# An fp32 encoder layer: one 512-column matmul for two of 256 in the up-projection, and one sum of weights made by an accumulating DMA

## The chip, the core and the metric

The kernel runs on one core of one Trainium2 chip. The metric is the device time in microseconds of one execution; the times are medians over several runs. One further execution was taken with the hardware profiler, and every duration, wait and start in this text comes from it. TensorE (PE in the profile) multiplies matrices, with its weight loads on a row of their own (PEld); VectorE (DVE) and ScalarE (ACT) work element by element and alone read TensorE's results out of PSUM; SyncE (SP) and GpSimd (POOL) issue the DMAs. Each engine works through a queue of its own, in order.

## The reference

One encoder layer on 512 tokens of 2048 channels, all in fp32: a normalisation and an input projection, a convolution group and a neighbourhood-attention group side by side, an output projection added to the residual, and then the part that the change touches, a gated feed-forward network with a width-3 depthwise convolution:

```
xn = rms_norm(x, ffn_norm_g[l])
up = jnp.einsum("bsd,df->bsf", xn, w_up[l])              # 2048 -> 2 x 5632
up = depthwise_conv(up, ffn_dw_w[l], ffn_dw_b[l])
gate, val = jnp.split(up, 2, axis=-1)
x = x + jnp.einsum("bsf,fd->bsd", jax.nn.silu(gate) * val, w_down[l])
return rms_norm(x, final_norm_g)
```

The shapes: `x` (1, 512, 2048), `w_up` (2048, 11264), `w_down` (5632, 2048).

## The kernel before

Activations lie with channels on the 128 partitions and the 512 tokens along the free axis, as tiles of 128x512 (`t2`, a pool of 79 buffers). TensorE multiplies fp32 numbers in two parts: a weight block of 128x1024 is split into a high part `whi` (a ScalarE copy, L108) and a low part `wlo` (a VectorE subtraction, L109), and `mm3` (L119 to L121) adds three products: high by high, high by low, low by high. The split blocks have three buffers each; `plan` lists all blocks in order, and `weights()` makes the splits two blocks ahead of the one in use. The raw blocks come through SP's DMA queue into nine buffers of 512 KB (`raw`).

The feed-forward network goes over 44 blocks `f` of 128 hidden channels, in 11 chunks of four (`NCH`, `CH`). For one `f` the gate and the value of all tokens are a product of 2x2 blocks: the weights are split by gate or value and by the parity of the channel tile (`a11`, `a21`, `a22`, `a12`), the activations by the parity of the channel tile and by token half. `up(f)` computes it with seven products instead of eight, of 256 columns each (`H` = 256 tokens). The seven right factors are sums of activations, made once and held split into high and low halves of one 128x512 tile (`comb`, the tiles `xc`, L488 to L491). The seven left factors are made per `f` in `factors`: three of the loaded blocks as they are, and four sums that VectorE adds (L531, L533, L535, L537), three of them in one buffer `ws`. A product is 8 accumulation steps of three matmuls. Its result lies in PSUM (`pu`, 3 buffers, the seventh product in another), is read by ScalarE copies (L576, L577) and VectorE adds (L578 to L585), and makes gate `g` and value `v`. `hidden(f)` scales both (L599, L600; the value's sign is turned there), applies the convolution (`conv3`, one ScalarE pass and two VectorE passes each), silu and the final product (L603).

The down-projection of a chunk runs during the next chunk. After the four `f` of a chunk, `in_two` splits each hidden tile into high and low (`hh`, `hl`, L608 and L609). `down` takes blocks of `w_down` in units; a unit makes two output tiles of 12 matmuls of 512 columns each (`pd`, two PSUM buffers), ScalarE copies each out (`pdc`, L621), and GpSimd issues a DMA that adds it to the running sum in DRAM (`x2d`, L622). In chunk 0 there is no down unit; in chunks 1 to 9 two units follow the seven products of each `f`; in chunk 10 two follow the second `f`, two the third and four the last. A last part multiplies the last chunk's hidden tiles and normalises.

The order of instructions on each engine is made by a scheduler when the kernel is built; pool buffers are handed out as they come free.

Of the kernel before, what the change touches and what calls it, by code (L numbers as in the profile page):

```python
# [30 lines left out]
KD = D // P  # L31
NC_ = CONV // P
NP_ = HEADS // 2
NF = FF // P
U = 8
# [5 lines left out]
H = S // 2  # L41
CH = 4
NCH = NF // CH
# [11 lines left out]
POFF = {}  # L55
# [8 lines left out]
def layer(ctx: ExitStack, tc: tile.TileContext, xT, w_in, w_out, w_up, w_down, par, tab, out):  # L64
    nc = tc.nc
    consts = ctx.enter_context(tc.tile_pool(name="consts", bufs=1))
# [4 lines left out]
    psm = ctx.enter_context(tc.tile_pool(name="psm", bufs=3, space=bass.MemoryType.PSUM))  # L71
# [10 lines left out]
    def t2(name, dt=F32):  # L82
        return tp.tile([P, S], dt, tag="t2k", name=name)

    def t4(shape, name):

        return wpool.tile(shape, F32, tag="raw", name=name, bufs=NR)

    prm = consts.tile([P, NPAR], F32, name="prm")
    nc.sync.dma_start(prm, par)  # L90

    def pc(name, i):
        o = POFF[name] + i
        return prm[:, o:o + 1]
# [6 lines left out]
    def raw_unit(src, n):  # L101
        raw = t4([P, U * P], "raw")
        return raw, nc.sync.dma_start(raw[:, :n], src)

    def parts(raw, n):
        hi = wpool.tile([P, U * P], F32R, tag="whi", name="whi")
        lo = wpool.tile([P, U * P], F32R, tag="wlo", name="wlo")
        i = nc.scalar.activation(hi[:, :n], raw[:, :n], AF.Copy)  # L108
        j = nc.vector.tensor_sub(lo[:, :n], raw[:, :n], hi[:, :n].bitcast(F32))  # L109
        return hi, lo, i, j  # L110

    def unit(src, n):

        return parts(raw_unit(src, n)[0], n)[:2]

    def mm3(ps, w, wk, mh, ml, start, stop):
        hi, lo = w[:2]
        a = slice(wk * P, (wk + 1) * P)
        nc.tensor.matmul(ps, hi[:, a], mh, start=start, stop=False)  # L119
        nc.tensor.matmul(ps, hi[:, a], ml, start=False, stop=False)  # L120
        return nc.tensor.matmul(ps, lo[:, a], mh, start=False, stop=stop)  # L121
# [100 lines left out]
    for step in ORDER:  # L222
        i = next(a_ if step == "a" else q_)
# [207 lines left out]
    p, n = -1, 0  # L431
# [52 lines left out]
    comb = [[] for _ in range(7)]  # L484

    def halves(src, c):

        t = t2("xc", F32R)  # L488
        nc.scalar.activation(t[:, :H], src, AF.Copy)
        nc.vector.tensor_sub(t[:, H:], src, t[:, :H].bitcast(F32))  # L490
        comb[c].append((t[:, :H], t[:, H:]))  # L491

    def after(d, ps):

# [23 lines left out]

    rstd2 = []

    def stats2():
        rstd2.append((yield from rsqrt_steps(acc2, D, "rstd2")))

    def factors(f):

        def make(c):
            if c == 0:
                a[:] = [raw_unit(w_up[f, q], U * P)[0] for q in range(4)] + [t4([P, U * P], "ws")]
            a11, a21, a22, a12, s_ = a
            if c == 1:  # L530
                add(s_, a21, a22)  # L531
            elif c == 2:
                add(s_, s_, a11)  # L533
            elif c == 4:
                add(a21, a21, a11)  # L535
            elif c == 5:
                add(s_, s_, a12)  # L537
            return parts((a11, s_, s_, a12, a21, s_, a22)[c], U * P)[:2]

        a = []  # L540
        return [lambda c=c: make(c) for c in range(7)]

    add = nc.vector.tensor_add

    def down_units(c, i):

        at = [0, 4, 8, 12, 16] if c < NCH - 1 else [0, 0, 4, 8, 16]
        return range(at[i], at[i + 1], U // CH) if c else ()

    def down_weights(f0, d0):  # L550
        return w_down[:, (f0 * KD + d0 * CH) * P:(f0 * KD + d0 * CH + U) * P]

    for c in range(NCH):
        for i in range(CH):
            plan.extend(factors(c * CH + i))
            for d0 in down_units(c, i):
                plan.append(lambda c=c, d0=d0: unit(down_weights((c - 1) * CH, d0), U * P))

    out_half(mb, after)
    steps.append(stats2())  # L560

    def up(f):

        def product(c):
            w = weights()
            ps = (psa.tile([P, S], F32, tag="po", name="pu") if c == 6 else
                  psm.tile([P, S], F32, tag="mm", name="pu"))[:, :H]
# [5 lines left out]
        uu, vv = t2("u"), t2("v")  # L573
        u, t, u2 = uu[:, :H], uu[:, H:], vv[:, :H]
        g, v = t2("g"), t2("vl")
        nc.scalar.activation(u, product(0), AF.Copy)  # L576
        nc.scalar.activation(t, product(1), AF.Copy)  # L577
# [6 lines left out]
        add(g[:, H:], t, product(5))  # L584
        add(v[:, :H], u2, product(6))  # L585
        return g, v

    def conv3(a, n):
        y = t2("uy")
        o = POFF["fww"] + 3 * n  # L590
        nc.scalar.activation(y, a, AF.Identity, scale=prm[:, o + 1:o + 2], bias=pc("fwb", n))
        nc.vector.scalar_tensor_tensor(y[:, 1:], a[:, :S - 1], prm[:, o:o + 1], y[:, 1:], op0=ALU.mult, op1=ALU.add)
        nc.vector.scalar_tensor_tensor(y[:, :S - 1], a[:, 1:], prm[:, o + 2:o + 3], y[:, :S - 1],
                                       op0=ALU.mult, op1=ALU.add)
        return y

    def hidden(f):
        g, v = up(f)
        nc.vector.tensor_mul(g, g, rstd2[0])  # L599
        nc.vector.scalar_tensor_tensor(v, v, -1.0, rstd2[0], op0=ALU.mult, op1=ALU.mult)  # L600
        g, v = conv3(g, f), conv3(v, NF + f)
        nc.scalar.activation(g, g, AF.Silu)
        nc.vector.tensor_mul(g, g, v)  # L603
        return g

    def in_two(g):
        h, l = t2("hh", F32R), t2("hl", F32R)
        nc.scalar.activation(h, g, AF.Copy)  # L608
        nc.vector.tensor_sub(l, g, h.bitcast(F32))  # L609
        return h, l  # L610

    def down(hs, ds):

        for d0 in ds:
            w = weights()
            for d in range(d0, d0 + U // CH):
                ps = psa.tile([P, S], F32, tag="tr", name="pd", bufs=2)
                for k in range(CH):
                    mm3(ps, w, (d - d0) * CH + k, *hs[k], k == 0, k == CH - 1)
                t = t2("pdc")  # L620
                nc.scalar.activation(t, ps, AF.Copy)  # L621
                nc.gpsimd.dma_start(xd[d], t, accum_op=ALU.add)  # L622
# [12 lines left out]
    x2 = []  # L635
# [95 lines left out]
```

## Time and profile before

| | before |
|---|---|
| median of 3 runs | 2103.06 us (2101.43 to 2103.21) |
| the profiled execution | 2101.72 us, span 2099.9 us, granted TensorE clock 0.996 |
| PE / PEld / DVE / ACT / POOL busy | 98% / 88% / 76% / 47% / 7% of the span |
| DMA | 270.90 MB, 129 GB/s over the span |
| feed-forward network | from about 705 us of the span on |

The span runs from the first to the last instruction. "Busy" for TensorE counts each matmul from its start to its modelled end, and matmuls overlap, so neither its share nor its mean is the price of one more matmul; starts in the timeline give that. In a row of a group, the numbers after the first bar are busy time and the mean in ns of one instruction; after the second bar stands the idle time before them and what ended it. In a timeline row the first two numbers are start and length in us, and a bracket at its end gives the idle time before and who ended it. In a row by stretches the engines' busy times stand in the order PE, PEld, DVE, ACT, POOL, then the granted clock, the share of the DMA engines and GB/s.

### The profile page before, as it was taken

The numbers are of one execution on the slowest core, as the hardware profiler recorded it, in microseconds if no ns is written. First come the engines' busy times: TensorE is split into PE (matmuls) and PEld (weight loads), VectorE is DVE, ScalarE is ACT, GpSimd is POOL, SyncE is SP. The second block draws the span as 40 slices with busy tenths as digits, with TensorE's granted clock in tenths as the row PEclk, the third lists the DMA queues.
The fourth block names the chain that finished last, engine by engine and source line by source line (L and its number), as shares of the span: only waits on it lengthen the run. The fifth ranks groups of instructions, "written<-read, shape, count | busy, mean of one in ns | idle before, by whom it ended". The sixth has DMA issues, their size and how long they took to land.

```text
span 2099.9 us, 32453 instructions
## 1 busy us (share of the span) xinstructions
PE 2061.7 (98%) x13024; PEld 1851.1 (88%) x13024; DVE 1585.8 (76%) x2180; ACT 985.3 (47%) x1428; POOL 140.0 (7%) x166
## 2 busy tenths in 40 slices
PE   8999999999999999999999999999999999999997
PEld 6888888877778899999999999999999999999987
DVE  7985796686568898777777778777777777878756
ACT  6234424447436544444444444454454444545452
POOL 0000000000000000110110110110111011010110
PEclk9999999999999999999999999999999999999998
DMA  6333223335324244555555565665565555554672
GB/s 237 101 111 110 81 81 110 101 101 200 116 96 140 71 121 124 138 130 143 130 139 143 122 146 135 132 140 136 137 140 127 144 131 138 144 121 123 147 193 81
DMA packets 95911, 270.90 MB, mean 129 GB/s; under 512 B 10640, under 2 KB 14736, under 8 KB 95760
## 3 DMA queue, kind: packets, MB, share of 16 engines
q1 hardware_dynamic: 72720, 226.88, 33.7%
q0 software_dynamic: 23040, 41.95, 14.7%
q8 instruction: 102, 1.67, 0.3%
q14 instruction: 49, 0.40, 0.1%
HBM read 218.46 MB, written 50.33 MB: 128 GB/s over the span
## 4 chain that ended last, share of the span: by engine, by line
PE 94%; DVE 4%; DMA 1%; ACT 1%; issue 0%; SPq 0%; DVEq 0%; ACTq 0%
PE pu L121 13%; PE pu L119 13%; PE pu L120 13%; PE pd L119 8%; PE pd L120 8%; PE pd L121 8%; PE pj L119 7%; PE pj L121 7%; PE pj L120 7%; PE po L119 2%; PE po L120 2%; PE po L121 2%; DVE wlo L109 1%; PE sc L365 1%; PE po L408 1%; PE trp L395 1%
## 5 line engine op out<-in xcount | busy, mean ns | idle before, releaser
L121 PE MATMUL pu<-xc,wlo 128*128 128x256 f32 x2464 | 697.8, 283 | 2.1 <-DVE wlo L109 2.1
L108 ACT ACTIVATE whi<-raw 128x1024 fp32r<-128x1024 f32 x368 | 389.4, 1059 | 660.0 <-PE pu L120 299.3
L119 PE MATMUL pu<-xc,whi 128*128 128x256 f32 x2464 | 698.3, 283 | 0.8 <-ACT whi L108 0.7
L120 PE MATMUL pu<-xc,whi 128*128 128x256 f32 x2464 | 698.0, 283 | 0.0
L109 DVE TENSOR_TENSOR wlo<-raw,whi 128x1024 fp32r<-128x1024 f32 x368 | 449.1, 1222 | 171.6 <-ACT whi L108 143.9
L121 PEld LDWEIGHTS pu<-xc,wlo 128*128 128x128 f32 x2464 | 473.3, 192 | 3.2 <-DVE wlo L109 3.2
L119 PEld LDWEIGHTS pu<-xc,whi 128*128 128x128 f32 x2464 | 473.5, 192 | 2.9 <-ACT whi L108 1.2
L120 PEld LDWEIGHTS pu<-xc,whi 128*128 128x128 f32 x2464 | 473.6, 192 | 1.9 <-issue 0.2
L109 DVE TENSOR_TENSOR wlo<-ws,whi 128x1024 fp32r<-128x1024 f32 x132 | 161.5, 1223 | 160.2 <-ACT whi L108 159.7
L622 POOL DMA_DIRECT2D x2d<-pdc x160 | 139.3, 873 | 1896.0 <-ACT pdc L621 1893.4
L119 PE MATMUL pj<-xh,whi 128*128 128x512 f32 x640 | 254.1, 398 | 8.5 <-ACT whi L108 8.5
L121 PE MATMUL pj<-xh,wlo 128*128 128x512 f32 x640 | 250.3, 391 | 1.7 <-DVE wlo L109 1.7
L119 PE MATMUL pd<-hh,whi 128*128 128x512 f32 x640 | 249.6, 390 | 1.9 <-ACT pdc L621 1.9
L120 PE MATMUL pj<-xl,whi 128*128 128x512 f32 x640 | 250.3, 391 | 0.0
L108 ACT ACTIVATE whi<-ws 128x1024 fp32r<-128x1024 f32 x132 | 139.9, 1060 | 233.7 <-PE pd L120 142.4
L120 PE MATMUL pd<-hl,whi 128*128 128x512 f32 x640 | 249.5, 390 | 0.0
L121 PE MATMUL pd<-hh,wlo 128*128 128x512 f32 x640 | 249.0, 389 | 0.0
L279 DVE SCALAR_TENSOR_TENSOR y<-ch,prm,y 128x504 f32<-128x504 f32 (+14 forms) x240 | 170.2, 741 | 3.2
L119 PEld LDWEIGHTS pj<-xh,whi 128*128 128x128 f32 x640 | 120.7, 189 | 37.0 <-ACT whi L108 10.5
L121 PEld LDWEIGHTS pj<-xh,wlo 128*128 128x128 f32 x640 | 120.5, 188 | 29.1 <-DVE wlo L109 3.6
L119 PEld LDWEIGHTS pd<-hh,whi 128*128 128x128 f32 x640 | 120.3, 188 | 26.3 <-ACT pdc L621 2.3
L121 PEld LDWEIGHTS pd<-hh,wlo 128*128 128x128 f32 x640 | 120.1, 188 | 25.3
(141 smaller groups left out, 2403.4 us busy)
## 6 DMA issues: line engine op xcount, KB each, us to landing
raw<-in_w_up SPq DMA_DIRECT2D x176, 512.0 KB, 4.1
raw<-in_w_down SPq DMA_DIRECT2D x88, 512.0 KB, 3.7
raw<-in_w_in SPq DMA_DIRECT2D x80, 512.0 KB, 3.6
x2d<-pdc POOLq DMA_DIRECT2D x160, 256.0 KB, 4.2
raw<-in_w_out SPq DMA_DIRECT2D x32, 512.0 KB, 3.5
x<-in_xT SPq DMA_DIRECT2D x32, 256.0 KB, 6.0
tab<-in_tab SPq DMA_DIRECT2D x32, 256.0 KB, 4.0
x2d<-x SPq DMA_DIRECT2D x16, 256.0 KB, 2.0
```

What stands on the lines that cost most here:

```text
L108: i = nc.scalar.activation(hi[:, :n], raw[:, :n], AF.Copy)
L109: j = nc.vector.tensor_sub(lo[:, :n], raw[:, :n], hi[:, :n].bitcast(F32))
L119: nc.tensor.matmul(ps, hi[:, a], mh, start=start, stop=False)
L120: nc.tensor.matmul(ps, hi[:, a], ml, start=False, stop=False)
L121: return nc.tensor.matmul(ps, lo[:, a], mh, start=False, stop=stop)
L279: nc.vector.scalar_tensor_tensor(y[:, a:b], h[:, a + j - PAD:b + j - PAD], prm[:, o + j:o + j + 1], y[:, a:b], op0=ALU.mult, op1=ALU.add)
L365: m = nc.tensor.matmul(both[:, j, i, :], q[hp, b * P:(b + 1) * P], grid(k, KC0[b], KW)[hp], start=True, stop=True)
L395: m = nc.tensor.transpose(ps[:, 2 * i + ch, :], s[:, i, ch * P:(ch + 1) * P], ident)
L408: m = nc.tensor.matmul(grid(po, b * BLK, BLK)[hp], vt[b // 2][:, 2 * (b % 2) + ch, hp], pts[j][:, 2 * i + ch, :], start=(ch == 0), stop=(c ...
L622: nc.gpsimd.dma_start(xd[d], t, accum_op=ALU.add)
```

## The change

Five edits, all in the feed-forward network:

- `up`: the high weights meet the whole tile `xc` (high and low halves, 512 columns) in one matmul, and the low weights meet its high half (256 columns) and are added to the second half of the result. The matmuls per accumulation step go from three to two; in the last step the wide one comes second.
- The two halves of each result are then added: ScalarE copies the second half (`low_part`), VectorE adds both to what it combined before. Some adds are joined over 512 columns.
- `factors`: the sum of `a21` and `a22` is no longer made by VectorE. `a21` is loaded a second time, into the buffer of the sum, and a DMA issued by GpSimd adds `a22` to it from DRAM. The other three sums stay.
- The down units move: in chunks 1 to 9 one follows the fourth product and one the seventh, instead of both following the seventh (`between`, `down_units` with `at`).
- The value's sign is turned by negated convolution weights (`fwn`, made once) rather than at the scaling.

```
@@ factors
-                a[:] = [raw_unit(w_up[f, q], U * P)[0] for q in range(4)] + [t4([P, U * P], "ws")]
+                a[:] = [raw_unit(w_up[f, q], U * P)[0] for q in (0, 1, 2, 3, 1)]
+                nc.gpsimd.dma_start(a[4], w_up[f, 2], accum_op=ALU.add)
             a11, a21, a22, a12, s_ = a
-            if c == 1:
-                add(s_, a21, a22)
-            elif c == 2:
+            if c == 2:
                 add(s_, s_, a11)
@@ down_units, and plan
-    def down_units(c, i):
-        at = [0, 4, 8, 12, 16] if c < NCH - 1 else [0, 0, 4, 8, 16]
-        return range(at[i], at[i + 1], U // CH) if c else ()
+    def down_units(c, i, at):
+        n = U // CH
+        if not c:
+            return ()
+        if c < NCH - 1:
+            return {3: (4 * i,), 6: (4 * i + n,)}.get(at, ())
+        return {(1, 3): (0,), (1, 6): (2,), (2, 3): (4,), (2, 6): (6,), (3, 6): range(8, KD, n)}.get((i, at), ())
...
@@ up
-            for k in range(U):
-                m = mm3(ps, w, k, *comb[c][k], k == 0, k == U - 1)
-            tick(m)
-            return ps
+            for k in range(U):
+                hi, lo = (w[i][:, k * P:(k + 1) * P] for i in range(2))
+                m = comb[c][k]
+                wide = lambda: nc.tensor.matmul(ps, hi, m, start=k == 0, stop=k == U - 1)
+                low = lambda: nc.tensor.matmul(ps[:, H:], lo, m[:, :H], start=False, stop=False)
+                if k < U - 1:
+                    wide()
+                    i = low()
+                else:
+                    low()
+                    i = wide()
+            tick(i)
+            between(c)
+            return ps[:, :H], ps[:, H:]
+        def low_part(ps):
+            t = t2("pl")[:, :H]
+            nc.scalar.activation(t, ps, AF.Copy)
+            return t
-        nc.scalar.activation(u, product(0), AF.Copy)
-        nc.scalar.activation(t, product(1), AF.Copy)
-        add(u2, u, product(2))
-        add(t, t, u2)
-        add(g[:, :H], u, product(3))
-        ps = product(4)
-        add(u2, u2, ps)
-        add(v[:, H:], t, ps)
-        add(g[:, H:], t, product(5))
-        add(v[:, :H], u2, product(6))
+        m, l = product(0)
+        add(u, m, low_part(l))
+        m, l = product(1)
+        add(t, m, low_part(l))
+        m, l = product(2)
+        l = low_part(l)
+        add(u2, u, m)
+        add(u2, u2, l)
+        add(t, t, u2)
+        low = t2("pl")
+        m, l = product(3)
+        nc.scalar.activation(low[:, :H], l, AF.Copy)
+        add(g[:, :H], u, m)
+        m, l = product(4)
+        add(u, m, low_part(l))
+        add(v.rearrange("p (i t) -> p i t", i=2), uu, u.unsqueeze(1).broadcast_to([P, 2, H]))
+        m, l = product(5)
+        nc.scalar.activation(low[:, H:], l, AF.Copy)
+        add(g[:, H:], t, m)
+        add(g, g, low)
+        m, l = product(6)
+        l = low_part(l)
+        add(v[:, :H], v[:, :H], m)
+        add(v[:, :H], v[:, :H], l)
@@ hidden
-        nc.vector.scalar_tensor_tensor(v, v, -1.0, rstd2[0], op0=ALU.mult, op1=ALU.mult)
+        nc.vector.tensor_mul(v, v, rstd2[0])
@@ the loop over chunks
         for i in range(CH):
-            hs.append(hidden(c * CH + i))
-            if c == NCH - 1 and i == CH - 1:
-                hs = [in_two(h) for h in hs]
-            down(pend, down_units(c, i))
-        pend = hs if c == NCH - 1 else [in_two(h) for h in hs]
+            last = c == NCH - 1 and i == CH - 1
+            hs.append(hidden(c * CH + i, lambda at: None if last else down(pend, down_units(c, i, at))))
+        hs = [in_two(h) for h in hs]
+        if last:
+            down(pend, down_units(c, i, 6))
+        pend = hs
```

As built, the queue orders differ in one more way that the prediction uses: at the start of chunks 2 to 9 the scheduler puts nine of the down unit's matmuls ahead of the fourth product of the first `f`, and on VectorE's queue all four `hl` subtractions ahead of the read of that `f`'s first product.

More of the change, by code (lines that the diff above doesn't have):

```diff
@@ L519, in layer @@
     rstd2 = []
+    fwn = consts.tile([P, 3 * NF], F32, name="fwn")
+    nc.vector.tensor_scalar(fwn, prm[:, POFF["fww"] + 3 * NF:POFF["fww"] + 6 * NF], -1.0, None, op0=ALU.mult)
     def stats2():
@@ L554, in layer, with up @@
         for i in range(CH):
-            plan.extend(factors(c * CH + i))
-            for d0 in down_units(c, i):
-                plan.append(lambda c=c, d0=d0: unit(down_weights((c - 1) * CH, d0), U * P))
+            for at, make in enumerate(factors(c * CH + i)):
+                plan.append(make)
+                for d0 in down_units(c, i, at):
+                    plan.append(lambda c=c, d0=d0: unit(down_weights((c - 1) * CH, d0), U * P))
     out_half(mb, after)
     steps.append(stats2())
-    def up(f):
+    def up(f, between):
         def product(c):
@@ L566, in product @@
             ps = (psa.tile([P, S], F32, tag="po", name="pu") if c == 6 else
[L567 removed]
+                  psm.tile([P, S], F32, tag="mm", name="pu"))
             for k in range(U):
[L569 to L576 removed]
@@ L590, in conv3, with hidden @@
         o = POFF["fww"] + 3 * n
-        nc.scalar.activation(y, a, AF.Identity, scale=prm[:, o + 1:o + 2], bias=pc("fwb", n))
-        nc.vector.scalar_tensor_tensor(y[:, 1:], a[:, :S - 1], prm[:, o:o + 1], y[:, 1:], op0=ALU.mult, op1=ALU.add)
-        nc.vector.scalar_tensor_tensor(y[:, :S - 1], a[:, 1:], prm[:, o + 2:o + 3], y[:, :S - 1],
+        w, o = (prm, o) if n < NF else (fwn, o - POFF["fww"] - 3 * NF)
+        nc.scalar.activation(y, a, AF.Identity, scale=w[:, o + 1:o + 2], bias=pc("fwb", n))
+        nc.vector.scalar_tensor_tensor(y[:, 1:], a[:, :S - 1], w[:, o:o + 1], y[:, 1:], op0=ALU.mult, op1=ALU.add)
+        nc.vector.scalar_tensor_tensor(y[:, :S - 1], a[:, 1:], w[:, o + 2:o + 3], y[:, :S - 1],
                                        op0=ALU.mult, op1=ALU.add)
         return y
-    def hidden(f):
-        g, v = up(f)
+    def hidden(f, between):
+        g, v = up(f, between)
         nc.vector.tensor_mul(g, g, rstd2[0])
-        nc.vector.scalar_tensor_tensor(v, v, -1.0, rstd2[0], op0=ALU.mult, op1=ALU.mult)
+        nc.vector.tensor_mul(v, v, rstd2[0])
         g, v = conv3(g, f), conv3(v, NF + f)
```

7 lines of the change are left out of this document (6 added, 1 removed).

## The prediction

> **What bounds the kernel now.** I read the page's busy shares and chain first, then what TensorE waited for, then the timeline of TensorE and VectorE in the up-projection, since every edit is there.
>
> ```profile
> span 2099.9 us, 32453 instructions
> PE 2061.7 (98%) x13024; PEld 1851.1 (88%) x13024; DVE 1585.8 (76%) x2180; ACT 985.3 (47%) x1428; POOL 140.0 (7%) x166
> PE 94%; DVE 4%; DMA 1%; ACT 1%; issue 0%; SPq 0%; DVEq 0%; ACTq 0%
> L121 PE MATMUL pu<-xc,wlo 128*128 128x256 f32 x2464 | 697.8, 283 | 2.1 <-DVE wlo L109 2.1
> ```
>
> The chain is TensorE's (PE's). Of the up-projection's three lines of 2464 matmuls each, the one that multiplies the low part waits 2.1 us in all. A mean of 283 ns overlaps its neighbours (three lines of 698 us would fill the span alone), so the price of a matmul must be read from starts:
>
> ```profile
> 1006.71 0.39 PE L119 MATMUL pd<-hh,whi 128*128 128x512 f32 x1
> 1006.94 0.39 PE L120 MATMUL pd<-hl,whi 128*128 128x512 f32 x1
> 1007.16 0.39 PE L121 MATMUL pd<-hh,wlo 128*128 128x512 f32 x1
> 1007.39 0.28 PE L119 MATMUL pu<-xc,whi 128*128 128x256 f32 x1
> ...
> 1007.98 0.28 PE L121 MATMUL pu<-xc,wlo 128*128 128x256 f32 x1
> 1008.10 0.28 PE L119 MATMUL pu<-xc,whi 128*128 128x256 f32 x1
> 1024.86 0.42 DVE L584 TENSOR_TENSOR g<-u,pu 128x256 f32<-128x256 f32 x1 [0.68 <-PE pu L121]
> 1055.92 0.42 DVE L584 TENSOR_TENSOR g<-u,pu 128x256 f32<-128x256 f32 x1 [0.68 <-PE pu L121]
> ```
>
> 512 columns take 0.227 us from start to start (0.68 over three), 256 columns 0.120 (0.12 at 1007.98, and all between). L584 comes once per f: 31.06 us apart, and 168 x 0.120 + 48 x 0.2267 is 31.04. So in a steady f TensorE is fed without a gap, and only its own instruction stream counts. A line through the two prices has 13.3 ns that do not depend on the columns (2 x 0.120 - 0.2267).
>
> **The change, part by part.**
>
> *One wide matmul for two.* Three starts of 0.120 become 0.2267 + 0.120: 13.3 ns less, 2464 times, **-32.8 us**. The profile has no 512 beside a 256 with weights alternating, but pd-to-pu at 1007.16 is such a change and costs 0.23, no more. The Trainium skill, "TensorE: Matmul & The Clock Gate", section "Back-to-back issue gap", speaks against this: it gives a warm gap of N/2.4 + 2.5 ns, a fixed part of 2.5 ns only; by that the sum below has -6.2 in place of -32.8. The rows here, 0.120 where the page's formula has 0.109, disagree.
>
> *VectorE and ScalarE.* The wide result must be added to itself.
>
> ```profile
> L109 DVE TENSOR_TENSOR wlo<-raw,whi 128x1024 fp32r<-128x1024 f32 x154 | 188.3, 1223 | 47.8 <-ACT whi L108 47.7
> L108 ACT ACTIVATE whi<-raw 128x1024 fp32r<-128x1024 f32 x154 | 163.3, 1061 | 225.8 <-PE pu L120 193.4 <-issue 28.2 <-ACT hh L608 3.1
> L609 DVE TENSOR_TENSOR hl<-uy,hh 128x512 fp32r<-128x512 f32 x28 | 18.6, 684 | 0.0
> L621 ACT ACTIVATE pdc<-pd 128x512 f32<-128x512 f32 x104 | 61.1, 588 | 41.9 <-PE pd L121 41.9
> L591 ACT ACTIVATE uy<-vl,prm 128x512 f32<-128x512 f32 x25 | 20.4, 817 | 0.0
> L608 ACT ACTIVATE hh<-uy 128x512 fp32r<-128x512 f32 x28 | 15.9, 619 | 0.0
> L577 ACT ACTIVATE u<-pu 128x256 f32<-128x256 f32 x26 | 9.5, 366 | 0.0
> 1025.32 0.69 DVE L599 TENSOR_TENSOR g<-g,rstd 128x512 f32<-128x512 f32 x1
> 1025.93 1.22 DVE L109 TENSOR_TENSOR wlo<-raw,whi 128x1024 fp32r<-128x1024 f32 x1
> 1027.06 0.75 DVE L592 SCALAR_TENSOR_TENSOR uy<-g,prm,uy 128x511 f32<-128x511 f32 x1
> 1027.74 0.42 DVE L585 TENSOR_TENSOR vl<-v,pu 128x256 f32<-128x256 f32 x1
> 1028.08 0.74 DVE L593 SCALAR_TENSOR_TENSOR uy<-g,prm,uy 128x511 f32<-128x511 f32 x1
> 869.60:1180.00 310.40, 310.40 (x2161) 291.46 (x2160) 234.52 (x282) 150.37 (x192) 34.81 (x40) 1.00 0.59 137
> ```
>
> Back to back, VectorE goes on after 1.14 (1024 wide), 0.67 (conv), 0.61 (512) and 0.34 us (256). Per f, one sum of weights goes (-1.14), seven combining adds become ten of 256 and two of 512 (+3 x 0.34 + 2 x 0.61 = +2.2): +1.1 us. The last row has ten f: 23.45 us of VectorE and 15.0 of ScalarE per f; they become some 24.6 and 16.9 (five more copies of 0.37) of the new period, 168/3 x 0.3467 + 48 x 0.2267 = 30.3 us. Both stay below it, so in the middle of a chunk the adds cost nothing if none is late. I walked the queue order of the changed program with these prices, T = 0 at the end of an f's second down unit, where c0 of the next f starts (a product is 8 x 0.3467 = 2.77). The split of c2 waits for that unit's weight buffer: ScalarE to 1.03, VectorE 1.07 to 2.2. Then stand c6's add (2.2), a conv step (2.6, when ScalarE has done a down copy 0.59, a PSUM copy 0.37 and the conv's first term 0.82), an add (3.3), a conv step (3.6), the scaling (4.3), c3's split (4.9 to 6.1), a conv step (6.0), and at 6.7 the read of c0's PSUM, done 7.1. Product c3 takes c0's PSUM buffer and starts at 3 x 2.77 = 8.3: 1.2 us to spare, **0**. The split of the down unit between c3 and c4 is done at 9.9, due at 11.1. The sign that moves from L600 into the conv weights, and the one negation at the start (0.2), are nothing.
>
> *At a chunk's start* four `hl` subtractions (L609's form, 0.61 from start to start) are queued ahead of that read. On the same walk: c3's split 6.1, conv 6.75, hl, conv, hl, final product, hl (9.8), split of the down unit (11.0), hl, and only then c0's read, done 11.9. TensorE's order there puts nine matmuls of the down unit before c3; four can run (8.3 to 9.2), the fifth needs the down unit's low part (11.0), so c3 starts at 12.15 rather than 10.36: 1.8 us. Before, down came after all seven products, so 10.9 us of matmuls covered this. Chunks 2 to 9: **8 x 1.8 = +14.3**. In the first f of chunk 10 no down unit lies beside it: c3 at 11.96 rather than 8.32, and some 0.9 in the next f: **+4.5**. Bounds for one: 0 (the hl's run in the 2.5 us that VectorE idles before T = 0; the queue order excludes a gain) to 4.3 (the read at 11.9 with nothing of the down unit early and 0.7 of hand-overs).
>
> *Chunk 0*, without down units, is VectorE's already:
>
> ```profile
> 765.16 0.42 DVE L584 TENSOR_TENSOR g<-u,pu 128x256 f32<-128x256 f32 x1 [0.63 <-PE pu L121]
> 785.85 0.42 DVE L584 TENSOR_TENSOR g<-u,pu 128x256 f32<-128x256 f32 x1 [0.63 <-PE pu L121]
> 795.86 0.39 PE L121 MATMUL pu<-xc,wlo 128*128 128x256 f32 x1 [1.18 <-DVE wlo L109]
> ```
>
> 20.69 where 168 x 0.120 is 20.16. With 1.1 us more of VectorE it goes to about 20.9, where the wide matmuls would allow 19.4; the gap in the third row becomes some 2.3. Against the -32.8, which counts these f too: **+2.2** (0 to 5).
>
> *The accumulating DMA.* Per f one more 512 KB load and one accumulation of 512 KB into SBUF, issued by GpSimd (POOL).
>
> ```profile
> q1 hardware_dynamic: 72720, 226.88, 33.7%
> q0 software_dynamic: 23040, 41.95, 14.7%
> raw<-in_w_up SPq DMA_DIRECT2D x176, 512.0 KB, 4.1
> x2d<-pdc POOLq DMA_DIRECT2D x160, 256.0 KB, 4.2
> 1000.43 0.86 POOL L622 DMA_DIRECT2D x2d<-pdc  x1 [21.31 <-ACT pdc L621]
> ```
>
> By q1, 0.524 MB take 1.6 us of all sixteen engines; by q0, 3.9. Together 5.5 of 30.3 us: the share rises from 0.59 to about 0.77, still below 1. The order is what could cost. On SP's queue the new load stands behind a12's and ahead of the down weights and the next f's blocks, which are wanted nearly a period later: 0. The down units' loads keep their places; their copies (ScalarE) and accumulations (GpSimd) move apart with the units, two after c3 and two after c6: 0. The sum's buffer is the one that the f before used for a21, free after c4's split (T = 11.6, walk above). Load 4.1, GpSimd 0.9 (behind the first down tile's accumulation, which waits for its own copy at 14.8; the next tile's waits behind the sum, and only its own SBUF tile with it), landing 4.1 to 8.4 (the plain load; the 256 KB accumulation doubled); I take 8.4, it is the nearer kind: 25.0. ScalarE wants it when c6's weight buffer comes free, at 25.0, and VectorE then has 2.5 us of idle time before the next c2: **0**. An accumulation that lands late holds ScalarE and VectorE, in whose queues the next splits and reads stand behind it.
>
> Sum: -32.8 + 14.3 + 4.5 + 2.2 = -11.8. The profiled execution took 2101.72, 1.82 outside the span; it becomes 2089.9. The median of the runs, 2103.06, lies 1.3 above it: **2091**.
>
> **Rivals.** *The DMA closes a loop (slower).* From that split (ScalarE 1.1, VectorE 12.5 to the end of c4's split), load 4.1 and GpSimd 0.9, back to it: 18.6 us beside the landing, so at a landing above 11.7 us the loop is longer than 30.3 and each us more costs 39. At 16.8 (four times the row above): +199, 2290; at 14: +90, 2181. For: an accumulation beside a busier set of queues; q0 moves a byte 2.4 times as dearly as q1. Against: it needs nearly three times the row. 0.13.
> *No stall at the chunks' starts*, if VectorE runs ahead of my walk: -32.8 + 2.2, 2072. Against: the order is fixed and the reads stand last. 0.11.
> *Larger stalls*: 8 x 4.3 + 6 + 5 = +45, 2116. For: each hand-over between engines adds up along twelve steps. 0.12.
> *The fixed 13.3 ns do not go with the removed matmul*: if only 2.5 ns of it do, -6.2 + 21 gives 2118. The rows of two widths speak against it. This is the skill's formula named above. 0.03.
> *The change does nothing on TensorE* (weights not held over 512 columns): pd rows do it. 0.01.
>
> **How the numbers follow.** Forecast 0.60, its own range 2083 to 2100 (stalls of 0.8 to 2.9). The range 2072 to 2116 takes in the cases without stalls and with larger ones, and leaves out the loop and the edges. A measurement tells 0.2%, 4.2 us, from no change. Faster: 0.55 of the forecast and 0.11, 0.66. Slower: 0.13 + 0.11 + 0.03, 0.27. Same: 0.07.
>
> **What would show it.** The wide matmul 0.227 and the narrow 0.120 from start to start; an f within a chunk 30.3 us; at each chunk's start a wait of TensorE's down matmul for VectorE's split of about 1.8; f in chunk 0 at 20.9; the accumulation landing below 11.7. I am wrong if f within a chunk exceeds 30.5, with TensorE, ScalarE or VectorE waiting for the accumulated sum; or if the narrow matmul grows beside the wide.

## The result: slower, 2181.52 us against 2102.62

The changed kernel takes 2181.52 us (median of 4 runs, 2179.06 to 2189.01), the kernel before 2102.62 beside it: a ratio of 1.0382, 95% interval [1.0356, 1.0408]. The forecast was 2091, its range 2072 to 2116. The profiled execution, the slowest of the four (2189.01), has a span of 2187.2 us, 87.3 more than before; the medians differ by 78.9.

The page of the changed kernel, in the order in which the prediction read the page of before: span, busy shares, chain, the wide matmul, the one sum of weights that lies inside `a21`, and the DMA rows.

```profile
span 2187.2 us, 28151 instructions
PE 2082.5 (95%) x10560; PEld 1736.6 (79%) x10560; DVE 1617.9 (74%) x2357; ACT 1025.6 (47%) x1648; POOL 179.5 (8%) x210
PE 65%; DVE 18%; DMA 9%; issue 4%; ACT 3%; DVEq 0%; ACTq 0%; SPq 0%
L579 PE MATMUL pu<-xc,whi 128*128 128x512 f32 x2464 | 880.4, 403 | 30.6 <-DVE u L603 30.6
L537 DVE TENSOR_TENSOR raw<-raw 128x1024 f32<-128x1024 f32 x44 | 53.9, 1225 | 135.1 <-DMA raw<-in_w_up 135.1
raw<-in_w_up SPq DMA_DIRECT2D x220, 512.0 KB, 4.4
raw<-in_w_up POOLq DMA_DIRECT2D x44, 512.0 KB, 8.8
```

TensorE's share of the chain fell from 94% to 65%; VectorE and DMA came in. The wide matmul waits 30.6 us for L603, the read of c0's PSUM buffer (c0 to c6 are the seven products of an `f`, in order). L537 (`a21 += a11`, for c4) stood still 135 us for a load: VectorE, 74% busy, is not the bound by its work but by its order. The accumulation lands in 8.8 us; the estimate was 8.4.

What TensorE and ScalarE waited for, in the changed kernel (total, times, longest):

```profile
PE pu L579 <- DVE u L603: 30.6, 25, 3.4
PE pd L121 <- DVE wlo L109: 20.7, 9, 2.5
PE pd L119 <- ACT whi L108: 14.6, 8, 2.1
ACT whi L108 <- DVE raw L535: 139.6, 37, 5.5
ACT whi L108 <- DMA raw<-in_w_up: 89.4, 30, 4.0
```

The first row lies in the middle of the chunks, except for its longest wait, which is in chunk 10's first `f`; the next two lie at the chunks' starts. L614, which reads product c3, runs once per `f`. Its starts over a chunk's start and two steady `f` of the changed kernel:

```profile
1173.95 0.42 DVE L614 TENSOR_TENSOR g<-u,pu 128x256 f32<-128x256 f32 x1
1211.40 0.41 DVE L614 TENSOR_TENSOR g<-u,pu 128x256 f32<-128x256 f32 x1
1242.55 0.42 DVE L614 TENSOR_TENSOR g<-u,pu 128x256 f32<-128x256 f32 x1
1275.15 0.42 DVE L614 TENSOR_TENSOR g<-u,pu 128x256 f32<-128x256 f32 x1
```

37.45, 31.15 and 32.60 us, where 31.06 stood before. The mean over chunks 1 to 9 is 31.96 within a chunk (27 intervals) and 37.69 across the starts of chunks 2 to 9 (8); in chunk 0 it is 20.6. Now the chain of the changed kernel in one of these `f`, in order of time (start, length, what):

```profile
1244.79 1.23 DVE wlo L109
1246.03 7.57 DMA raw<-in_w_up
1253.76 1.08 issue
1254.84 1.23 DVE wlo L109
1256.09 1.24 DVE raw L535
...
1264.14 0.35 DVE u L603
1264.53 0.50 PE pu L579
```

A split frees a weight buffer at 1246.0, and SP issues into it the load of `a21` for the `f` two ahead of the one that TensorE works on. The load takes 7.57 us. L537 of that later `f` (the chain's "issue" at 1253.76) stands in VectorE's queue some 43 us ahead of the split of c4 that needs it (1297.3), and waits until the load has landed; behind it stand a split, L535 (whose sum ScalarE must split for c2), convolution steps and at last L603, for which TensorE waits at 1264.5. L537's row, and why the load took 7.57, in GpSimd's timeline and the DMA share of the same stretch:

```profile
1253.69 1.23 DVE L537 TENSOR_TENSOR raw<-raw 128x1024 f32<-128x1024 f32 x1 [4.27 <-DMA raw<-in_w_up]
1243.69 0.89 POOL L532 DMA_DIRECT2D raw<-in_w_up  x1 [3.26 <-DMA raw<-in_w_up]
1244.00:1248.00 4.00, 4.00 (x24) 3.45 (x23) 3.40 (x6) 1.97 (x3) 1.49 (x2) 1.00 0.98 246
1248.00:1252.00 4.00, 4.00 (x21) 3.35 (x20) 1.43 (x2) 0.30 (x1) 0.00 (x0) 1.00 0.99 238
1242.55:1275.15 32.60, 30.89 (x162) 26.14 (x161) 23.43 (x33) 15.11 (x23) 4.88 (x6) 1.00 0.66 163
```

The sum is the last of an `f`'s five loads, so its accumulation begins just as SP starts on the first two loads of the `f` after it. For 8 us the DMA engines are full (share 0.98 and 0.99, the second column from the end), while the whole `f` (last row) has 0.66. The prediction reasoned with the average, 0.77, and below 1; this stretch was not.

One `f` later it is the sum itself. GpSimd waits for its load, and ScalarE's split for c1 for its landing:

```profile
1274.67 0.88 POOL L532 DMA_DIRECT2D raw<-in_w_up  x1 [1.59 <-DMA raw<-in_w_up]
1283.41 1.06 ACT L108 ACTIVATE whi<-raw 128x1024 fp32r<-128x1024 f32 x1 [3.35 <-DMA raw<-in_w_up]
```

A chunk's start, TensorE's two long waits and the granted clock (the column before the last two):

```profile
1061.88 0.50 PE L119 MATMUL pd<-hh,whi 128*128 128x512 f32 x1 [2.05 <-ACT whi L108]
1065.57 0.80 PE L121 MATMUL pd<-hh,wlo 128*128 128x512 f32 x1 [2.50 <-DVE wlo L109]
1066.00:1068.00 2.00, 2.00 (x6) 1.52 (x6) 2.00 (x5) 0.00 (x0) 0.00 (x0) 0.50 0.70 176
1068.00:1070.00 2.00, 2.00 (x8) 1.71 (x7) 2.00 (x4) 0.00 (x0) 0.00 (x0) 0.50 0.51 145
1070.00:1072.00 2.00, 2.00 (x10) 1.71 (x10) 0.05 (x1) 0.00 (x0) 0.00 (x0) 0.80 0.83 264
```

4.55 us of waits, with four matmuls between them, and then 5.2 us of work at half clock (until about 1070.8), which loses 2.6 more: 7.2 of the 8.2 us by which this interval (38.79) is above the 30.63 of an undisturbed `f` (below). On the mean of the eight it is 37.69 - 30.63 = 7.06.

Where the 87.3 us lie, cut at the reads of product c3 (`f` counted from 0):

| stretch | before | changed | difference |
|---|---|---|---|
| up to the first read (f0) | 717.0 | 718.3 | +1.2 |
| f0 to f3 (chunk 0) | 64.5 | 61.9 | -2.6 |
| f3 to f4 | 21.8 | 28.5 | +6.7 |
| f4 to f39 (chunks 1 to 9) | 1086.1 | 1164.4 | +78.2 |
| f39 to f43 (chunk 10) | 112.7 | 112.9 | +0.1 |
| the rest | 97.8 | 101.4 | +3.6 |

Two rows have to be read together. From f3 to f4 the changed kernel runs 24 matmuls of a down unit that ran after the read of f4 before; at 0.2267 they are 5.4 of the +6.7. From f39 to f43 it has 24 fewer in turn, so the +0.1 there stands for some 5.5 us of loss: TensorE's wait of 3.41 us for L603 in chunk 10's first `f`, and the half clock that follows.

### The profile page after: what moved, and what is told of

It reads as the page before. It is cut to its first block, busy times and chain, and to the rows that moved or that the text cites. A ratio compares the mean times of both kernels' runs of the same rounds, so it can differ in the third digit from the quotient of the medians.

```text
span 2187.2 us, 28151 instructions
## 1 busy us (share of the span) xinstructions
PE 2082.5 (95%) x10560; PEld 1736.6 (79%) x10560; DVE 1617.9 (74%) x2357; ACT 1025.6 (47%) x1648; POOL 179.5 (8%) x210
## 4 chain that ended last, share of the span: by engine, by line
PE 65%; DVE 18%; DMA 9%; issue 4%; ACT 3%; DVEq 0%; ACTq 0%; SPq 0%
PE pu L579 13%; DMA raw<-in_w_up 9%; DVE wlo L109 7%; PE pu L580 7%; PE pj L119 6%; PE pj L121 6%; PE pj L120 6%; PE pd L121 5%; PE pd L119 5%; PE pd L120 5%; PE po L119 3%; PE po L120 3%; PE po L121 3%; DVE uy L634 2%; ACT whi L108 2%
## 5 line engine op out<-in xcount | busy, mean ns | idle before, releaser
L579 PE MATMUL pu<-xc,whi 128*128 128x512 f32 x2464 | 880.4, 403 | 30.6 <-DVE u L603 30.6
L108 ACT ACTIVATE whi<-raw 128x1024 fp32r<-128x1024 f32 x500 | 527.1, 1056 | 810.0 <-PE pj L120 213.0
L109 DVE TENSOR_TENSOR wlo<-raw,whi 128x1024 fp32r<-128x1024 f32 x500 | 609.9, 1221 | 257.6 <-ACT whi L108 232.7
L580 PE MATMUL pu<-xc,wlo 128*128 128x256 f32 x2464 | 648.5, 284 | 1.9 <-DVE wlo L109 1.8
L579 PEld LDWEIGHTS pu<-xc,whi 128*128 128x128 f32 x2464 | 457.6, 191 | 130.2 <-DVE u L603 36.2
L121 PE MATMUL pd<-hh,wlo 128*128 128x512 f32 x640 | 254.2, 399 | 20.7 <-DVE wlo L109 20.7
L119 PE MATMUL pd<-hh,whi 128*128 128x512 f32 x640 | 256.4, 401 | 18.1 <-ACT whi L108 14.6
L537 DVE TENSOR_TENSOR raw<-raw 128x1024 f32<-128x1024 f32 x44 | 53.9, 1225 | 135.1 <-DMA raw<-in_w_up 135.1
L120 PEld LDWEIGHTS pd<-hl,whi 128*128 128x128 f32 x640 | 122.3, 191 | 25.8
L120 PEld LDWEIGHTS pj<-xl,whi 128*128 128x128 f32 x640 | 120.6, 189 | 24.6 <-issue 0.7
L663 ACT ACTIVATE pdc<-pd 128x512 f32<-128x512 f32 x160 | 93.3, 584 | 46.8 <-PE pd L121 46.3
```

The lines of the kernel that those rows point to most:

```text
L579: wide = lambda: nc.tensor.matmul(ps, hi, m, start=k == 0, stop=k == U - 1)
L580: low = lambda: nc.tensor.matmul(ps[:, H:], lo, m[:, :H], start=False, stop=False)
```

## The experiments

**1. Parts of the change.** First with VectorE's L537 kept where c4 wants it, then with the sum back on VectorE.

```
e1, from the changed kernel          e2, from the changed kernel: in factors
-  add(a21, a21, a11)                -  for q in (0, 1, 2, 3, 1);  gpsimd.dma_start(a[4], ..., accum_op=ALU.add)
+  pin(add(a21, a21, a11))           +  for q in range(4);  t4([P, U * P], "ws") as the sum's buffer
                                     +  if c == 1: add(s_, a21, a22)
```

> The changed kernel with one instruction put elsewhere: VectorE's sum a21 + a11 stands in its queue where the program text has it (behind the sums of the third product), not a whole f earlier. Theory A (order): in the changed kernel this sum stands an f early and waits 135 us in all for the load of a21; with it late that wait is below 20 us, an f within a chunk falls from about 32.2 to 30.3 to 31, the starts of chunks still stall, 2095 to 2125. Rival B (traffic): the accumulating DMA keeps the DMA engines full, so another instruction waits for a load in its place; above 2155. Rival C (load): the combining adds alone make the read of the first product's PSUM late; 2170 to 2185, and the fourth product still waits for it in every f.

> The changed kernel with the sum a21 + a22 made by VectorE again: no second load of a21, no accumulating DMA. Everything else as changed. B (traffic): loads land in about 4 us again, the waits for loads go, 2085 to 2115. A (order): sums that stand an f early still wait for their loads, for some 4 us less than with the accumulation beside them, so 2110 to 2150. C (load): VectorE has 1.1 us more per f than the changed kernel, 2180 or more.

The late L537: 2182.74, ratio 1.0380 [1.0353, 1.0406], no gain in all; by the two profiles chunks 1 to 9 became 30 us shorter (1134.6 from f4 to f39), and chunk 0 13 us longer (74.7 from f0 to f3). L537's wait for the DMA is gone, and ScalarE's stand in its place:

```profile
ACT whi L108 <- DVE raw L537: 199.3, 43, 5.7
ACT whi L108 <- DMA raw<-in_w_up: 181.1, 39, 6.3
```

ScalarE's split of the accumulated sum now waits for its landing: the row has 181 us where it had 89, some nine tenths of it for the sum. Without the accumulation: 2113.73, ratio 1.0045 [1.0028, 1.0062]. So 68 of the 79 us go with the accumulating DMA. What is left has the shape of the prediction: steady 30.63, and at a chunk's start

```profile
PE pd L121 <- DVE wlo L109: 11.5, 8, 1.5
1030.73 0.41 DVE L615 TENSOR_TENSOR g<-u,pu 128x256 f32<-128x256 f32 x1
1063.13 0.41 DVE L615 TENSOR_TENSOR g<-u,pu 128x256 f32<-128x256 f32 x1
1093.76 0.41 DVE L615 TENSOR_TENSOR g<-u,pu 128x256 f32<-128x256 f32 x1
```

32.40 against 30.63: 1.77 us, eight times, where the walk gave 1.8. And the clock stays at full speed after it.

**2. The accumulation alone, and the wide matmul alone.**

```
e3, from the kernel before: in factors
-  for q in range(4);  t4([P, U * P], "ws")     +  for q in (0, 1, 2, 3, 1);  gpsimd.dma_start(a[4], ..., accum_op=ALU.add)
-  if c == 1: add(s_, a21, a22)
e4, from e2: the down units after the seventh product
-  hidden(c * CH + i, lambda at: ... down(pend, down_units(c, i, at)))
+  hidden(c * CH + i, lambda at: None);  down(pend, down_units(c, i))
```

> The kernel before with one part of the change: a21 loaded twice and a22 added to it by the accumulating DMA, instead of by VectorE. Matmuls, adds and down units as before. A (order): nothing stands early, TensorE stays fed, 2098 to 2110. B (traffic): loads take 8 us where the accumulation runs, TensorE waits; 2130 or more. C: VectorE has 1.1 us less per f, chunk 0 gains some 2 us: 2098 to 2104.

> The changed kernel with the sum a21 + a22 on VectorE and both down units behind the seventh product, as before: what is left of the change is the wide matmul, its combining adds and the turned sign. A and B: TensorE is fed as before and gains 13.3 ns on each of 2464 steps, chunk 0 loses some 5 us on VectorE; 2072 to 2085. C (load): VectorE's queue is late within each f also here, the fourth product waits; 2103 or more.

On the kernel before, the accumulation costs 4 us: 2107.85, ratio 1.0017 [1.0008, 1.0027]; it lands in 6.1. The wide matmul with grouped down units gives 2099.53, ratio 0.9981 [0.9971, 0.9990]. No part alone costs 68. Of e4's gain, 12.5 us between f4 and f39, most is lost again at the edges: 3.9 before the first read (only 1.0 in e10, which differs there by PSUM columns alone, so this part varies by execution), 5.5 from f3 to f4, 3.0 after the last.

**3. Is it the place of the down units, the traffic, the landing, or the `hl` subtractions?**

```
e5: e4 with the accumulating DMA                                 (down units grouped)
e6: changed kernel,  -  accum_op=ALU.add                         (a22 only loaded: the sum is left out)
e7: e2 with, per f,  +  nc.sync.dma_start(idle, w_up[f, 1])
                     +  nc.gpsimd.dma_start(idle, w_up[f, 2], accum_op=ALU.add)
e8: e2 with          +  hs.append(in_two(hidden(...)))           in place of four in_two at the chunk's end
```

> The changed kernel with the accumulating DMA kept, but both down units of an f after its seventh product, as before the change. Theory C (the accumulated sum costs only beside interleaved down units, because there the queues of VectorE and ScalarE have about 1 us of slack at the fourth product): 2104, that is the wide matmul alone (2099.5) and the 4 us that the accumulation cost on the kernel before; chunk starts 31 us, f 30.63. Theory A (the sum's DMA traffic, or its chain, costs wherever the down units stand): 2160 to 2185, f within a chunk 31 to 32.

> The changed kernel with GpSimd's DMA loading a22 into the sum's buffer instead of adding it (the sum is then a22 alone; bytes, waits and queue orders are those of the changed kernel). Theory A1 (what costs is that an accumulation holds the DMA engines 2.4 times as long for a byte and lands late): the landing falls from 8.8 to 4 to 5 us, and the time to 2115 to 2130. Theory A2 (what costs is the chain itself, one more buffer, load and second DMA that ScalarE and VectorE wait for): 2160 to 2185, as the changed kernel.

> The kernel of the second experiment (sum back on VectorE, 2113.7), with the load of a21 and the accumulation of a22 still made for every f, at the same places of the queues, but into an idle buffer that nothing reads (two activation buffers fewer make room for it). Theory T (traffic: the other loads land later for it): 2150 to 2185, raw loads landing at 4.5 to 5 in place of 3.9. Theory D (dependence: only the waiting for the sum costs): 2114 to 2120, f 30.63 and chunk starts 32.4 us.

> The kernel of the second experiment, with the hidden tile of each f split into high and low parts as soon as it is made, instead of four at the end of the chunk, so that one hl subtraction and not four stands ahead of the read of the first product. If the 1.8 us at each of eight chunk starts are those subtractions, as the prediction has it: 2113.7 - 8 x 1.8 = 2099, chunk starts 30.7 us. If they are only moved into the f's: 2113 to 2116.

| | sum on VectorE | sum accumulated by DMA |
|---|---|---|
| down units grouped | 2099.53 (e4) | 2105.43 (e5), ratio 1.0010 [1.0001, 1.0019] |
| down units interleaved | 2113.73 (e2) | 2181.52 (changed kernel) |

The cost is an interaction: 6 us beside grouped down units, 68 beside interleaved ones. It is not traffic as such: e7 moves the same bytes, at the same places of the queues, into a buffer that nobody reads, and takes 2114.45 (ratio 1.0053 [1.0038, 1.0068]), 0.7 us above e2, although that accumulation is as slow as the changed kernel's:

```profile
idle<-in_w_up POOLq DMA_DIRECT2D x44, 512.0 KB, 8.7
PE pd L121 <- DVE wlo L109: 11.7, 8, 1.6
1276.80 1.22 DVE L542 TENSOR_TENSOR raw<-raw 128x1024 f32<-128x1024 f32 x1
```

In e7 the accumulation delays a load of `a21` too (6.20 us from 1253.38 on, where e2 has 3.49), but L542, the add that is L537 in the changed kernel, starts at 1276.80, 17.2 us after that load has landed; in e2 as in e7 it waits for no load. So e7 takes away two things at once: ScalarE's wait for the sum, and a VectorE add that is first in line for the delayed load.

What counts is that queues wait. With a plain load in its place (e6) the landing falls to 6.4 and the time to 2140.38, ratio 1.0178 [1.0163, 1.0193]: 41 us with the landing's 2.4, and 27 left that the chain costs even so. Neither forecast for e6 was met; both had a share.

e8 missed: 2129.07, ratio 1.0126 [1.0109, 1.0143], and not 2099. The chunk starts did become like the other `f`, but all of them now take 31.14. In chunks 1 to 9 that is 3.8 us more than in e2 (35 x 0.5 lost, 8 x 1.77 won); most of the rest lies in chunk 0 (24.8 an `f`, 10.2 more from f0 to f3, 5.9 less from f3 to f4) and chunk 10 (6.4 more). The four `hl` subtractions were the chunk starts' stall, but one in every `f` costs as much and more. Which hand-over makes the 0.5 was not settled: TensorE's waits for L109 there add up to 6.4 us only.

**4. The price of a step, chunk 0, and one more buffer.**

```
e9:  e4, per product seven wide matmuls, eight narrow, one wide
e10: e4,  -  matmul(ps[:, H:], lo, m[:, :H])     +  matmul(ps[:, :H], lo, m[:, :H])
e11: e4 with the accumulating DMA only where f < CH (chunk 0)
e12: changed kernel,  -  NT = 79, NR = 9         +  NT = 77, NR = 10
```

> The wide matmul alone (fourth experiment, 2099.5), with each product's matmuls in another order: seven wide ones, eight narrow ones, one wide, so that the width changes twice in a product and not fifteen times. If a change of width is what made a step 0.3527 us in place of 0.3467 (13 changes fewer of 14 steps' 6 ns each): f 30.3 us and 2099.5 - 14 = 2086. If the 6 ns belong to the wide matmul with two kinds of weights, or to PSUM, whatever the order: 2099 to 2100, f 30.6.

> The wide matmul alone (2099.5), with the narrow matmul added to the first half of the PSUM tile instead of the second (the two halves are added later, so the result is the same). If the 6 ns of a step come from writing the PSUM columns that the wide matmul wrote last: f 30.3 and 2086. If not: 2099 to 2100, f 30.63.

> The wide matmul alone (2099.5), with the accumulating DMA for the four f of chunk 0 only, where VectorE is the bound (f 22.0 to 22.3 us there; 20.9 with the accumulation). Theory: 2 x 1.2 less in chunk 0, and 0 later: 2097. If the accumulation's landing is late there as well: 2100 to 2105.

> The changed kernel with ten raw weight buffers in place of nine (and two activation buffers fewer to make room), so that every load, a21's and the sum's among them, can be issued one buffer earlier. Theory D (what costs is the chain buffer, load, accumulation, split, which is longer than the buffers allow for): most of the 68 us go, 2115 to 2140, and the waits for the loads with them. Theory Q (the order of VectorE's queue costs, whatever the loads do): 2165 to 2185.

e10: 2100.02, ratio 0.9983 [0.9973, 0.9992], `f` 30.63: the PSUM columns do not matter. e9: 2089.81, ratio 0.9936 [0.9921, 0.9951], `f` 30.44: the change of width does, though for 0.19 us of an `f` rather than 0.33. The timelines, first of the changed kernel, then of e9:

```profile
1057.90 0.40 PE L579 MATMUL pu<-xc,whi 128*128 128x512 f32 x1
1058.14 0.28 PE L580 MATMUL pu<-xc,wlo 128*128 128x256 f32 x1
1058.26 0.40 PE L579 MATMUL pu<-xc,whi 128*128 128x512 f32 x1
```

```profile
1255.59 1.77 PE L575 MATMUL pu<-xc,whi 128*128 128x512 f32 x7
1257.20 1.11 PE L577 MATMUL pu<-xc,wlo 128*128 128x256 f32 x8
1258.15 0.40 PE L578 MATMUL pu<-xc,whi 128*128 128x512 f32 x1
1258.38 1.77 PE L575 MATMUL pu<-xc,whi 128*128 128x512 f32 x7
```

Alternating, a pair takes 0.36 here, in hundredths, and 0.3527 by the steady `f`: (30.63 - 48 x 0.2267) / 56. The starts of some 270 pairs in e2's trace, in ns, give 0.235 for the wide one and 0.117 for the narrow one. Sorted by width, seven wide ones take 1.61 (0.230 each) and eight narrow ones 0.95 (0.119 each): 0.349 a pair. By the steady `f` of e9, (30.44 - 48 x 0.2267) / 56, it is 0.3493. So 3.4 ns of the 6 go to the alternation; the rest is seen in the wide matmul, 0.230 rather than 0.2267, also when it stands among its own kind. Sorting by width also sorts by kind of weights, high or low; which of the two the alternation costs was not separated.

e11: 2095.34, ratio 0.9963 [0.9950, 0.9975]: in chunk 0, where VectorE is the bound and no down units run, the accumulation is worth 4 us, more than expected.

e12 missed theory D: 2178.33, ratio 1.0361 [1.0346, 1.0377]. Given one more buffer, the scheduler moved L537 one split further ahead, and its wait stayed (142 us in place of 135).

**5. Order and supply together.** VectorE's queue is the same in e1, e13, e15 and e16.

```
e13: e1 with NT = 77, NR = 10
e15: e1, loads of an f in the order a11, sum, a12, a21, a22:
     -  for q in (0, 1, 2, 3, 1);  gpsimd.dma_start(a[4], ...);  a11, a21, a22, a12, s_ = a
     +  for q in (0, 1, 3, 1, 2);  gpsimd.dma_start(a[1], ...);  a11, s_, a12, a21, a22 = a
e16: e15 with NT = 77, NR = 10
e17: e15 without the pin
e14: e9 with the accumulating DMA only where f < CH
```

> The first experiment (L537 kept late, 2182.7) with ten raw buffers in place of nine; VectorE's queue is unchanged by it. If the sum's landing, too late for c1's split, is what then cost the 68 us: the load is issued a buffer's life (about 4 us) earlier, ScalarE's wait of 181 us for the sum falls below 60, f within a chunk 30.63, and the time to 2120 to 2140. If something else holds the queues: 2170 to 2183.

> The first experiment (L537 kept late, 2182.7) with the loads of an f issued in the order in which its products want them: a11, the sum (a21 with a22 added), a12, a21, a22. VectorE's queue is unchanged by it. If the sum's landing costs the 68 us: the sum is loaded three places earlier, ScalarE's wait for it goes, and 2114 to 2130 is left (the second experiment's chunk starts). If only some of it: 2140 to 2165. If the other loads are now the late ones, or something else holds the queues: 2170 to 2190.

> The same with ten raw buffers too. If supply and order are the whole cause: no wait for a load is left, f within a chunk 30.63, chunk starts 32.4, and 2112 to 2118, the time of the second experiment. If more than 2130, a part of the cost is neither.

> The changed kernel with the loads of an f issued as a11, the sum, a12, a21, a22, and L537 where the scheduler puts it (ahead of its need, as in the changed kernel). If a VectorE queue that waits for a21's load is half of the cause: a21 now lands later still, L537's wait for it stays at 100 us or more, and the time at 2140 to 2180. If the late sum was all of it: 2110 to 2120, as with both.

> The wides first (2089.8) with the accumulating DMA in chunk 0 alone: the two gains lie in different stages, f 30.44 us from chunk 1 on and 20 to 21 in chunk 0 in place of 22.1 to 23.2: 2089.8 - 4.2 = 2085.6. If chunk 0 is then bound otherwise: 2089 to 2090.

| kernel | us | ratio |
|---|---|---|
| e13, L537 late, one more buffer | 2111.05 | 1.0032 [1.0020, 1.0044] |
| e15, L537 late, loads as wanted | 2110.04 | 1.0029 [1.0018, 1.0040] |
| e16, all three | 2110.63 | 1.0034 [1.0022, 1.0046] |
| e17, loads as wanted alone | 2110.33 | 1.0031 [1.0021, 1.0040] |

All four are some 3 us below e2 and below most of what was expected of them. From f4 to f39 they take 1086 to 1087 us, as e2 does, and from f0 to f4 91 to 92 where e2 takes 96.9: put rightly, the accumulation costs nothing and gains around chunk 0. That the VectorE add that it saves makes this gain was not tested apart. In e13 the accumulation still lands in 8.7 us, and the plain loads take 6.2 where the changed kernel has 4.4: with the add late and the loads a buffer earlier, slow transfers cost nothing. I had expected e17 to stay slow, and it did not: the change in the order of the loads alone, with the queues that the scheduler makes of it, is enough. Its rows:

```profile
DVE raw L537 <- DMA raw<-in_w_up: 18.2, 32, 2.6
PE pd L121 <- DVE wlo L109: 13.2, 9, 1.7
raw<-in_w_up POOLq DMA_DIRECT2D x44, 512.0 KB, 5.5
1252.69 0.87 POOL L532 DMA_DIRECT2D raw<-in_w_up  x1 [7.14 <-DMA raw<-in_w_up]
```

The sum is now the second load, its accumulation starts at 1252.69, after the burst in which SP loads for the next `f` (1243.69 in the changed kernel, at its beginning), and lands in 5.5 us rather than 8.8; L537 waits 18 us rather than 135, and TensorE's waits are nearly e2's. The same accumulation placed last in line met the loads that VectorE's next instruction needed. e17 takes away both waits at once, though: the sum comes early, `a21`, now fourth, is loaded after the accumulation (from 1266.50 on, in 3.5 us), and the scheduler put L537 26 us ahead of its split and not 43. How the 68 us divide between the two waits is therefore not shown; e1 and e12 show that neither the place of L537 nor a buffer more is enough by itself, and e15, with VectorE's queue of e1, that the order of the loads then is.

e14 puts together what helped: the wide matmul sorted by width, grouped down units, and the accumulation in chunk 0. 2083.50 us, ratio 0.9902 [0.9887, 0.9916], the fastest kernel of this study, `f` 30.44, and 19.5 to 20.7 in chunk 0.

## Why the prediction was wrong

- **The wide matmul, -32.8.** Right in sign, mis-sized. A steady `f` went from 31.06 to 30.63 where nothing else disturbed it (e2): 7.7 ns per step and not 13.3, which over 44 `f` would be -18.9. What failed in the term: 0.2267 for the wide matmul was read from `pd`, whose neighbours are as wide as it; alternating with narrow ones it costs 0.235, and the narrow one 0.117 in place of 0.120. The single row from `pd` to `pu` could not show 6 ns in a column of hundredths. The fixed-price rival (2.5 ns) was as far off on the other side.
- **Chunk starts, +14.3.** Right by itself: e2 has 1.77 for 1.8. In the changed kernel it is 7.06 (+56), since the late splits lengthen the same stall and then the clock halves.
- **In the middle of a chunk, 0.** The walk gave 1.2 us to spare at c3, and without the accumulation (e2) every such `f` took 30.63 to 30.64. It had no L537 in it, and left the load for L537 at its usual 4.1; the changed kernel has 1.32 us per `f` (31.96 - 30.63), 36 us over 27 `f`.
- **The accumulating DMA, 0.** This is the step that failed, and the largest part of the miss: 68 of the 90 us between the forecast and the time go with it, 14 with the wide matmul. The landing was right (8.4; it took 8.8), and the average share was below the forecast (0.66). What was wrong is "the down weights and the next f's blocks, which are wanted nearly a period later: 0." One of those blocks, `a21`, is wanted by L537 as soon as it can land, and the accumulation falls into the same 8 us and takes the load from 4.1 to 7.6. The zero for the sum itself failed too: it lands after ScalarE wants it (89 us of waits, and 181 in e1, where L537 does not wait). Runs e15 and e17 show that with the sum loaded second the same accumulation costs nothing; how much each of the two waits cost stays open. The sign of being wrong that the prediction named, an `f` above 30.5 with an engine waiting for the sum, came true (31.96).
- **Chunk 10, +4.5.** Right: TensorE's wait there is 3.41 us (3.40 in e2), where the walk had 11.96 - 8.32 = 3.64. The half clock that follows was not in it.
- **Chunk 0, +2.2.** 20.9 per `f` was forecast and 20.6 measured (61.88 / 3), so no loss there. Of the +6.7 from f3 to f4 some 1.3 are left beside the down unit that moved; in e4, where no unit moved, it is 5.5, with a wait of TensorE of 3.64 us for L599 (at 806.57), a read of PSUM. The tail grew by 3.6 (3.0 in e4); TensorE's wait ahead of the last part is 3.55 where it was 1.93. The prediction had no term for these two edges; that the added reads on VectorE and ScalarE cause them was not tested.
- **The loop rival** had a part of it. The landing stayed below its threshold of 11.7, but that threshold rested on loads of 4.1 us and on splits that come when the walk has them; with L537's waits ahead of the splits, ScalarE waits for the sum too (89 us), and with L537 out of the way for the sum above all (e1, 181 us). That the time equals the rival's 2181 is chance: it stood there for a landing of 14.
- **Not in the prediction: the clock.** Waits were priced at their length. The granted clock of the two profiled executions:

```profile
core 0: 2187.2 us, clock 0.979
core 0: 2111.8 us, clock 0.993
```

The first is the changed kernel, the second e2. 2187.2 x 0.021 = 46 and 2111.8 x 0.007 = 15 us of clock are missing: up to 31 of the 75 us between these two executions (an upper bound: part of it fell on idle time). The Trainium skill, "TensorE: Matmul & The Clock Gate", section "What's actually happening", states that the clock halves after an idle window of about 3.4 us and returns after a busy one of that length. The trace agrees in part: the half clock at 1064.0 lasted 6.8 us, about twice that length, and came back under work; but no wait there was 3.4 us long, only 2.05 and 2.50 with 1.2 us of matmuls between them. e2's waits at the chunk starts, 1.5 at the longest, were not followed by half clock, and neither was the single wait of 3.64 us in e4 (granted clock 1.00 from 803 to 809), so in these traces the length of a wait alone does not decide it.

Of the 75 us between e2 and the changed kernel, 27 x 1.32 = 36 lie within chunks 1 to 9 and 8 x 5.30 = 42 at chunk starts; the other stretches of the table give 3 back.

## What to carry to other kernels

An added transfer is not priced by its share of the DMA engines over a period, but by what else is in flight when it starts and which queue's next instruction needs that: find the load that it delays, and the instruction that stands first in line for it; where none does, as in e7, the delay was free. A stage that keeps 1 us to spare, as here after the down units were interleaved, turns such a delay into a wait in full, and in the changed kernel waits of 2 us and more close together cost a halved clock on top. Load in the order in which the products want the data, and read a matmul's price beside the neighbours that it will have.

## What the runs showed of the hardware that was not expected

- A 512-column matmul between 256-column ones took 0.235 us from start to start and the 256-column one 0.117 (e2); sorted by width they took 0.230 and 0.119 (e9). In the down units 512 columns took 0.227, and in the kernel before 256 columns 0.120.
- After 4.55 us of waits within 6 us the granted clock fell to 0.50 for about 6.8 us (changed kernel); e2, with 1.5 us of waits at the same places, kept 1.00, and so did e4 through one wait of 3.64 us.
- An accumulation of 512 KB landed in 5.5 us (e17), 5.9 (e5), 6.1 (e3), 7.4 (e12), 8.8 (changed kernel) or 9.5 (e1), with the same bytes; a plain load in the same place took 6.4 (e6).
